# A hybrid decoder layer on one core: each 512-column product pass issued as two passes of 256 columns

## The chip, the cores and the metric

The kernel runs on one core of a Trainium2 chip. The metric is the device time of one execution, in microseconds (us). The profile is that of one execution; "span" is its time from the first to the last instruction. TensorE multiplies (its matrix multiplies stand in the profile as PE, its loads of the stationary operand as PEld), VectorE is DVE, ScalarE is ACT, GpSimd is POOL, and SyncE (SP) issues the DMAs.

## What is computed

One layer with a residual stream of 1024 tokens by 1024 features, all in float32:

```python
xn = rms_norm(h, mix_norm)
z  = xn @ W_in                  # q | k | v | gate_a | u | gate_s, 512 columns each
attn = dilated_mixture_attention(q, k, v) * silu(gate_a)       # 8 heads of 64
ssm  = s5_glu(u, ...) * silu(gate_s)        # 32 groups, 64 complex states, then a GLU
h  = h + concat(attn, ssm) @ W_out
h  = h + sigmoid(rms_norm(h, ple_norm) @ W_g) * (p @ W_p)
```

## The kernel before

Every dense product of two float32 operands is made of three passes, so that the rounding of one pass is made up by the others. Each operand is split into a high part (a copy in float32r, on ACT, L157 for weights) and a low part (the difference, on DVE or POOL, L158 for weights). The helper `mm3` (L106 to L109) then adds high x high, high x low and low x high in one PSUM bank of 512 float32 columns. Its arguments are the bank `o`, the stationary operand (`lh`, `ll`, 128 columns) and the moving operand (`rh`, `rl`, 512 columns). Every `matmul` becomes one load of the stationary operand and one multiply.

By the loops of the code `mm3` is called 696 times with 512 columns: 64 times for the state space input (tiles `u`), 128 for the two gates (`g`), 64 each for `q`, `k` and `v`, 32 for the GLU (`glu`), 64 for each half of the output projection (`os`, `oa`), 120 for the embedding gate (`gt`) and 32 for the embedding projection (`pe`). That is 2088 passes of 512 columns. Another 16 calls have 256 columns: the last feature tile of `gt` is cut into columns 0 to 512, 512 to 768 and 768 to 1024 (`LASTC`), so 48 passes of 256 columns stand at the end of the program.

The program runs through these stages: `u`; then the state space heads (many small DVE operations, a scan for each of the 32 groups in eight rounds, each round ending in the tile `xpv` on DVE, which PE multiplies into `yp` at L599 and, after a GELU on ACT, transposes at L608), with the 16 gate tiles `g` woven in, each of which DVE takes out of PSUM at L640; then `q` and `k`; then `v`, the GLU and the first half of the output projection `os`, with attention woven in (scores `sc` at L793 and L750, row minima on DVE at L780, exponentials on ACT at L803, a transposing DMA into `pt`, products `pv` at L818 and L824, and a transpose of each finished token block, `at`, at L763); then `oa`, and then `gt` and `pe`.

The order on each engine isn't written out by hand. The kernel is built by a scheduler that plays the program through with its own estimates of durations and lets each engine take what is ready first by them, with priorities given by hand. So a change in the number or size of the multiplies can move instructions on every engine. On the chip each engine keeps to the order that the scheduler left.

Of the kernel before, what the change touches and what calls it, by code (L numbers as in the profile page):

```python
# [58 lines left out]
PB = {"prb": (2, 2), "hl": (2, 2), "pt": (3, 2)}  # L59
# [18 lines left out]
def hybrid_layer(ctx: ExitStack, tc: tile.TileContext, a: dict, dbg=None):  # L78
    nc = tc.nc
    V, A, Q, T = nc.vector, nc.scalar, nc.gpsimd, nc.tensor  # L80
# [7 lines left out]
    def bank(tag, name, shape=(P, 512)):  # L88
        return ps.tile(list(shape), F32, tag=tag, name=name, bufs=BANKS[tag])
# [13 lines left out]
    yg_s = dr.tile([512, S], F32, name="yg_s")  # L103
    h_s = dr.tile([D, S], F32, name="h_s")

    def mm3(o, lh, ll, rh, rl, first, last):  # L106
        T.matmul(o, lh, rh, start=first, stop=False)  # L107
        T.matmul(o, lh, rl, start=False, stop=False)  # L108
        T.matmul(o, ll, rh, start=False, stop=last)  # L109

    def rsqrt(pool, v, shape, tag, steps=3):
        y = pool.tile(list(shape), I32, tag=tag + "y", name=tag + "y")
# [9 lines left out]

    ident = cp.tile([P, P], F32, name="ident")

# [1 line left out]
    wp = ctx.enter_context(tc.tile_pool(name="wp", bufs=4, side="right"))  # L126
    rp = ctx.enter_context(tc.tile_pool(name="rp", bufs=2, side="right"))
    ph1 = ExitStack()
# [63 lines left out]
    for k in range(KT):  # L192
# [15 lines left out]
        for j in range(6):  # L208
            f, n = divmod(j, 2)
# [13 lines left out]
    for k in range(KT):  # L223
        for n in range(2):
            mm3(acc[n], wu[k][0][:, 3 * P:], wu[k][1][:, 3 * P:], xh[k][:, n * 512:(n + 1) * 512],
                xl[k][:, n * 512:(n + 1) * 512], k == 0, k == KT - 1)
# [4 lines left out]
        stats(ss, "st1", rcol, rrow)  # L231
        V.tensor_tensor(rsq_, rcol, rcol, op=OP.mult)

# [1 line left out]
    def p16(name):  # L235
        return s1.tile([P, G, 16], F32, tag="p16", name=name, bufs=7)

# [28 lines left out]
    def named(n, shape=(P, G)):  # L266
        return s1.tile(list(shape), F32, name=n)
# [73 lines left out]
    are, aim = named("are"), named("aim")  # L341
# [28 lines left out]
    tt(w16, bre, bc(sci, 16), OP.mult)  # L370
    tt(bb, bb, w16, OP.add)

    # powers of A: PA = [Re; -Im], PB = [-Im; -Re]
    pa, pb = named("pa", (P, G, 9)), named("pb", (P, G, 9))
    for hf, (x0, y0) in enumerate(((1.0, 0.0), (0.0, -1.0))):
        hs = slice(hf * 64, hf * 64 + 64)
# [39 lines left out]
    tt(r8, r8, r8, OP.mult)  # L416
    tt(r8, r8, r8, OP.mult)

    # rotations e^{i 8 theta k}, k = 16 a + b; sine rows are [s; -s]
    e1c, e1s = csr, snr  # L420
    for j in range(3):
        e1c, e1s = csq(named(f"ec{j}"), named(f"es{j}"), e1c, e1s, norm=True)
# [27 lines left out]
    def feat_tile(w, f, n, tag, name):  # L450
        o = bank(tag, name)
        c = slice(n * 512, (n + 1) * 512)
        for k in range(KT):
            mm3(o, w[k][0][:, f * P:(f + 1) * P], w[k][1][:, f * P:(f + 1) * P],
                xh[k][:, c], xl[k][:, c], k == 0, k == KT - 1)
        return o
# [10 lines left out]
    for f in range(4):  # L467
        ust = [ev(f"ust{f}{e}", (P, 4, P)) for e in range(2)]
        for n in range(2):
            o = uraw[f][:, n * 512:(n + 1) * 512]  # L470
# [158 lines left out]
                ssm_store(f, ygt[f])  # L629
    sp.close()  # L630

# [1 line left out]
    for c0, dst in ((2560, sg_s), (1536, sa_s)):  # L633
        w = [load_w(wp, a["w_in"], k, c0, lo=GL) for k in range(KT)]
        for f in range(4):
            for n in range(2):
                o = feat_tile(w, f, n, "big", f"g{c0}{f}{n}")
# [5 lines left out]

    rrp.close()

# [1 line left out]
    kvp = ExitStack()  # L647
    def tok_tiles(w, bs, names, tag):
        os_ = [bank(tag, name) for name in names]
# [44 lines left out]
    for which, c0 in (("q", 0), ("k", 512)):  # L694
        w = [load_w(wp, a["w_in"], k, c0) for k in range(KT)]
        for bp in range(4):
# [3 lines left out]
            for b, o in zip(pair, tok_tiles(w, pair, [f"{which}{b}" for b in pair], QB[bp])):  # L700
                o = o.rearrange("p (h d) -> p h d", d=64)
# [14 lines left out]
            for b in (2 * bp, 2 * bp + 1):  # L716
# [10 lines left out]
                else:  # L727
# [1 line left out]
                    A.activation(hl[:, :, 0:64], raw, AF.Copy)  # L729
                    tt(hl[:, :, 64:128], raw, hl[:, :, 0:64], OP.subtract)  # L730
                    nc.sync.dma_start(ks[:, :, c], hl, transpose=True)
# [1 line left out]
    ma, ms_ = {}, {}  # L733

    def split(hi, lo, src, eng=Q):
# [138 lines left out]

    ph1.close()

# [1 line left out]
    rawp[0] = ctx.enter_context(tc.tile_pool(name="raw2", bufs=RAW[1], side="right"))  # L878
    mpx = ExitStack()
    mp = mpx.enter_context(tc.tile_pool(name="mp", bufs=6, side="right"))  # L880
# [20 lines left out]
    for n in range(2):  # L901
        c = slice(n * 512, (n + 1) * 512)
        ms_[n] = quad(f"msh{n}"), quad(f"msl{n}")
        for f in range(4):
            o = bank("big", f"glu{f}{n}")
# [14 lines left out]
                split(ms_[n][0][:, f], ms_[n][1][:, f], y, E[EM[f]])  # L920
            step(GS[4 * n + f])

# [1 line left out]
    def out_proj(part, src, scale, done):  # L924
        w = {}
        for sec in range(2):
# [64 lines left out]
    for sec in range(2):  # L991
        w = [load_w(wp, a["w_ple_gate"], k, sec * 512, gain=plen[:, k:k + 1]) for k in range(KT)]
        wq = [load_w(ep, a["w_ple_proj"], k, sec * 512, "pg", nbuf=24) for k in range(2)]
        for fi in range(4):
            f = sec * 4 + fi
            fs = slice(fi * P, (fi + 1) * P)
            last = f == 7
# [24 lines left out]
            if last:  # L1022
                proj()
                for c in LASTC:
                    o = bank("big" if c[0] % 1024 == 0 else "s", f"gt{f}{c[0]}")
# [21 lines left out]


def _w_in_columns():
    """The u section with the channels of a group ahead of its groups."""  # L1050
    n = np.arange(3072)
    n[2048:2560] = n[2048:2560].reshape(4, 8, 16).transpose(0, 2, 1).reshape(512)
    return n
# [24 lines left out]
def _layout(inputs):  # L1078
# [3 lines left out]
    def cols(v):  # L1082
# [6 lines left out]
        "ple_norm": cols(i["ple_norm"][0]),  # L1089
        "b_glu": cols(i["b_glu"][0]),  # L1090
        "w_in": c(i["w_in"][0][:, _w_in_columns()]),
        "w_glu": c(i["w_glu"][0]),
        "w_out": c(i["w_out"][0]),
# [32 lines left out]
```

## Time and profile before

| | |
|---|---|
| runs shown, us | 686.2, 688.59 (median), 693.06 |
| the profiled execution's span, us | 686.2 |
| PE busy | 92% of the span, 3836 multiplies |
| PEld busy | 72%, 3836 loads |
| DVE busy | 72% |
| ACT, POOL busy | 42%, 44% |
| mean granted clock of TensorE | 0.968 of 2.4 GHz |

Multiplies overlap each other in the pipeline and their ends are modelled, so a busy share of PE near 100% says that there is always one under way. The distance from one start to the next is what one costs in a dense row. A wait is put down to what came last before the waiting instruction could start.

### The profile page before, as it was taken

The numbers are of one execution on the slowest core, as the hardware profiler recorded it, in microseconds if no ns is written. First come the engines' busy times: TensorE is split into PE (matmuls) and PEld (weight loads), VectorE is DVE, ScalarE is ACT, GpSimd is POOL, SyncE is SP. The second block draws the span as 40 slices with busy tenths as digits, with TensorE's granted clock in tenths as the row PEclk, the third lists the DMA queues.
The fourth block names the chain that finished last, engine by engine and source line by source line (L and its number), as shares of the span: only waits on it lengthen the run. The fifth ranks groups of instructions, "written<-read, shape, count | busy, mean of one in ns | idle before, by whom it ended". The sixth has DMA issues, their size and how long they took to land.

```text
span 686.2 us, 10942 instructions
## 1 busy us (share of the span) xinstructions
PE 630.0 (92%) x3836; PEld 491.9 (72%) x3836; DVE 496.8 (72%) x1126; ACT 289.5 (42%) x553; POOL 302.0 (44%) x230
## 2 busy tenths in 40 slices
PE   9997799777879999999899789889999999999997
PEld 6875577566768788877677556566677888888786
DVE  6999999899998557767553998957944766626322
ACT  7532123445576624348434646534513455113100
POOL 3433825866775224234332845422432437342641
PEclk9999899998999999999999889989999999999999
DMA  7803612323444746754661868899987243015101
GB/s 257 241 7 109 209 38 76 105 79 93 77 92 92 167 69 125 159 86 125 161 122 48 216 147 148 213 192 191 217 226 244 94 152 124 15 63 165 50 32 61
DMA packets 158119, 87.25 MB, mean 127 GB/s; under 512 B 117232, under 2 KB 130416, under 8 KB 158064
## 3 DMA queue, kind: packets, MB, share of 16 engines
q1 hardware_dynamic: 158064, 86.56, 50.7%
q8 instruction: 30, 0.49, 0.3%
q14 instruction: 25, 0.20, 0.1%
HBM read 48.81 MB, written 17.27 MB: 96 GB/s over the span
## 4 chain that ended last, share of the span: by engine, by line
PE 46%; DVE 26%; DMA 12%; issue 7%; ACT 5%; POOL 2%; SPq 1%; DVEq 0%; ACTq 0%; POOLq 0%
PE gt L108 4%; PE gt L109 4%; PE gt L107 3%; DMA wr<-in_w_in 3%; DMA pt<-hl 3%; PE oa L107 2%; PE oa L109 2%; PE oa L108 2%; DVE tmp L270 2%; PE q L109 2%; PE q L107 2%; PE q L108 2%; DVE wl L158 2%; DVE p L780 2%; PE k L108 2%
## 5 line engine op out<-in xcount | busy, mean ns | idle before, releaser
L158 POOL TENSOR_TENSOR wl<-wr,wh 128x512 fp32r<-128x512 f32 x34 | 49.4, 1457 | 67.8 <-ACT wh L157 44.5
L157 ACT ACTIVATE wh<-wr 128x512 fp32r<-128x512 f32 x68 | 41.9, 626 | 51.4 <-DMA wr<-in_w_in 22.4
L810 POOL TENSOR_TENSOR hl<-p,hl 128x384 f16<-128x384 f32 (+2 forms) x34 | 38.9, 1148 | 53.9 <-ACT hl L807 27.1
L107 PE MATMUL g<-xh,wh 128*128 128x512 f32 x128 | 52.6, 411 | 7.3 <-DVE gate L640 5.5
L109 PE MATMUL g<-xh,wl 128*128 128x512 f32 x128 | 52.5, 410 | 5.3 <-DVE wl L158 5.3
L803 ACT ACTIVATE p<-p,st 128x384 f32<-128x384 f32 (+4 forms) x64 | 39.8, 622 | 39.1 <-DVE st L780 38.9
L108 PE MATMUL g<-xl,wh 128*128 128x512 f32 x128 | 52.0, 407 | 0.0
L108 PE MATMUL gt<-hl,wh 128*128 128x512 f32 (+1 forms) x136 | 51.7, 381 | 0.0
L107 PE MATMUL gt<-hh,wh 128*128 128x512 f32 (+1 forms) x136 | 51.7, 382 | 0.0
L109 PE MATMUL gt<-hh,wl 128*128 128x512 f32 (+1 forms) x136 | 51.2, 382 | 0.0
L158 DVE TENSOR_TENSOR wl<-wr,wh 128x512 fp32r<-128x512 f32 x34 | 34.8, 1025 | 19.1 <-ACT wh L157 14.0
L1016 ACT ACTIVATE gg<-gg 128x512 f32<-128x512 f32 (+1 forms) x17 | 10.1, 605 | 67.4 <-DVE gg L270 67.2
L1018 POOL TENSOR_TENSOR gg<-gg,hs 128x512 f32<-128x512 f32 x14 | 18.0, 1290 | 43.1 <-DVE gg L270 41.5
L107 PEld LDWEIGHTS g<-xh,wh 128*128 128x128 f32 x128 | 24.6, 192 | 13.7 <-DVE gate L640 6.5
L270 DVE TENSOR_TENSOR gg<-gt,rrow 128x512 f32<-128x512 f32 (+1 forms) x17 | 10.8, 656 | 32.7 <-PE gt L109 32.6
L109 PEld LDWEIGHTS g<-xh,wl 128*128 128x128 f32 x128 | 24.7, 193 | 12.0 <-DVE wl L158 6.6
L818 PE MATMUL pv<-vv,pt 128*128 128x64 f16 x504 | 24.4, 198 | 6.3 <-DMA pt<-hl 6.2
L818 PEld LDWEIGHTS <-pt 128*128 128x128 f16 x504 | 19.0, 101 | 14.8 <-DMA pt<-hl 8.9
L107 PEld LDWEIGHTS gt<-hh,wh 128*128 128x128 f32 x136 | 25.6, 188 | 5.5
L108 PEld LDWEIGHTS gt<-hl,wh 128*128 128x128 f32 x136 | 25.6, 188 | 5.4
L109 PEld LDWEIGHTS gt<-hh,wl 128*128 128x128 f32 x136 | 25.6, 188 | 5.4
L780 DVE CUSTOM_DVE_ANT_0 p<-sc,mask,gc 128x128 f32<-128x128 f32 (+3 forms) x56 | 24.3, 458 | 6.7 <-PE sc L793 3.2
(330 smaller groups left out, 1957.2 us busy)
## 6 DMA issues: line engine op xcount, KB each, us to landing
wr<-in_w_in SPq DMA_DIRECT2D x48, 256.0 KB, 2.9
xr<-in_x SPq DMA_DIRECT2D x16, 256.0 KB, 4.7
wr<-in_w_out SPq DMA_DIRECT2D x16, 256.0 KB, 3.3
xos<-in_x SPq DMA_DIRECT2D x16, 256.0 KB, 4.0
h_s<-xos SPq DMA_DIRECT2D x16, 256.0 KB, 3.4
xoa<-h_s SPq DMA_DIRECT2D x16, 256.0 KB, 2.8
wr<-in_w_ple_gate SPq DMA_DIRECT2D x16, 256.0 KB, 3.0
out_t<-gg SPq DMA_DIRECT2D x15, 256.0 KB, 2.0
```

The costliest lines, as they stand in the source:

```text
L107: T.matmul(o, lh, rh, start=first, stop=False)
L108: T.matmul(o, lh, rl, start=False, stop=False)
L109: T.matmul(o, ll, rh, start=False, stop=last)
L157: A.activation(hi, raw, AF.Copy)
L158: E[lo_on[k % len(lo_on)]].tensor_tensor(lo, raw, hi.bitcast(F32), op=OP.subtract)
L270: V.tensor_tensor(o, x, y, op=op)
L780: V.tensor_tensor_reduce(out, sc, msk, gm, init, op0=OP.add, op1=OP.min, accum_out=acc_[:, hd:hd + 1])
L803: A.activation(pb_, pb_, AF.Exp, bias=mx[:, hc], scale=-1.0, accum_out=dn[:, hc])
L810: E[LE[b][h0 % len(LE[b])]].tensor_tensor(hl[:, na:2 * na], pr_[:, 0:na], hl[:, 0:na], op=OP.subtract)
L818: T.matmul(pv[:, hd], pt[:, nf + i * nt + j + na * lp, :], vv[:, k0 + j, hd, lv, :], start=first, stop=end and not nf and j == n - 1 and l ...
L1016: A.activation(gt_, gt_, AF.Sigmoid)
L1018: (V if last else Q).tensor_tensor(gt_, gt_, hs, op=OP.add)
```

## The change

Where the output has 512 columns, `mm3` cuts the bank and the moving operand into two halves of 256 columns. Each of the three passes becomes two multiplies, the left half and the right half, which follow each other with the same stationary operand. Calls with fewer columns keep their three passes. A few comments go too, and all lines behind line 106 stand 13 lines lower.

```diff
+    def halves_of(x):
+        n = x.shape[1] // 2
+        return x[:, 0:n], x[:, n:2 * n]
+
     def mm3(o, lh, ll, rh, rl, first, last):
-        T.matmul(o, lh, rh, start=first, stop=False)
-        T.matmul(o, lh, rl, start=False, stop=False)
-        T.matmul(o, ll, rh, start=False, stop=last)
+        if math.prod(o.shape[1:]) != 512:
+            T.matmul(o, lh, rh, start=first, stop=False)
+            T.matmul(o, lh, rl, start=False, stop=False)
+            T.matmul(o, ll, rh, start=False, stop=last)
+            return
+        (o0, o1), (h0, h1), (l0, l1) = halves_of(o), halves_of(rh), halves_of(rl)
+        T.matmul(o0, lh, h0, start=first, stop=False)
+        T.matmul(o1, lh, h1, start=False, stop=False)
+        T.matmul(o0, lh, l0, start=False, stop=False)
+        T.matmul(o1, lh, l1, start=False, stop=False)
+        T.matmul(o0, ll, h0, start=False, stop=False)
+        T.matmul(o1, ll, h1, start=False, stop=last)
```

PE's program grows from 4804 to 6900 rows. The other engines keep their instructions, but in another order. Three places show it.

**The end of the state space heads, on PE.** The tiles `xpv_1681` (before) and `xpv_1873` (after) are those of the last scan round, and `yp` is the product that waits for them. Before, all 384 passes of the gates and 10 passes of `q` stand ahead of the first row with that `xpv`:

```order
L109 MATMUL g_2260<-xh_131,wl_1536_2054 128x512
L107 MATMUL q_2365<-wh_0_2318,xh_124 128x512
L108 MATMUL q_2365<-wl_0_2319,xh_124 128x512
L109 MATMUL q_2365<-wh_0_2318,xl_132 128x512
L107 MATMUL q_2365<-wh_0_2324,xh_125 128x512
L107 MATMUL q_2456<-wh_0_2318,xh_124 128x512
L108 MATMUL q_2456<-wl_0_2319,xh_124 128x512
L108 MATMUL q_2365<-wl_0_2325,xh_125 128x512
L109 MATMUL q_2365<-wh_0_2324,xl_133 128x512
L107 MATMUL q_2365<-wh_0_2330,xh_126 128x512
L109 MATMUL q_2456<-wh_0_2318,xl_132 128x512
L599 MATMUL yp_1699<-cp_1481,xpv_1681 128x128
```

In the changed program the last gate tile, `g_2812`, has only just begun there:

```order
L122 MATMUL g_2759<-xh_131,wl_1536_2438 128x256
L117 MATMUL g_2812<-xh_124,wh_1536_2395 128x256
L118 MATMUL g_2812<-xh_124,wh_1536_2395 128x256
L119 MATMUL g_2812<-xl_132,wh_1536_2395 128x256
L120 MATMUL g_2812<-xl_132,wh_1536_2395 128x256
L121 MATMUL g_2812<-xh_124,wl_1536_2396 128x256
L122 MATMUL g_2812<-xh_124,wl_1536_2396 128x256
L117 MATMUL g_2812<-xh_125,wh_1536_2401 128x256
L612 MATMUL yp_1891<-cp_1673,xpv_1873 128x128
```

Counted in passes of 512 columns from the start of the program, 586 stand ahead of this `yp` before and 555.5 after (192 of `u`, 360 of fifteen gate tiles, 3.5 of the last one): 30.5 fewer.

**The same place on DVE.** `gate` is a gate tile taken out of PSUM (L640 before, L653 after), `wl_0` is a low part of a weight of `q` (L158 and L171). Before:

```order
L640 TENSOR_TENSOR gate_2256<-g_2231,rrow 128x512
L578 SCALAR_TENSOR_TENSOR y_1673<-r_732,w_1669 128x128 x4
L584 MEMSET xpv_1681 128x4
L270 TENSOR_TENSOR xpv_1681<-y_1673,ec_1651 128x4x127
L158 TENSOR_TENSOR wl_0_2325<-wr_0_2322,wh_0_2324 128x512
L270 TENSOR_TENSOR xpv_1681<-xpv_1681,ysw_1678 128x4x127
L640 TENSOR_TENSOR gate_2285<-g_2260,rrow 128x512
```

After:

```order
L653 TENSOR_TENSOR gate_2755<-g_2706,rrow 128x512
L283 TENSOR_TENSOR w_1861<-w_1861,vs_1858 128x512
L591 SCALAR_TENSOR_TENSOR y_1865<-r_924,w_1861 128x128 x4
L597 MEMSET xpv_1873 128x4
L283 TENSOR_TENSOR xpv_1873<-y_1865,ec_1843 128x4x127
L283 TENSOR_TENSOR xpv_1873<-xpv_1873,ysw_1870 128x4x127
L653 TENSOR_TENSOR gate_2808<-g_2759,rrow 128x512
L171 TENSOR_TENSOR wl_0_2901<-wr_0_2898,wh_0_2900 128x512
```

From the start of the program to the last `xpv`, DVE has the same instructions in both programs but two: one `gate` and one `wl_0` have moved behind it.

**The end of attention, on PE.** `at` is the transpose of the last token block, `os` the first half of the output projection. Before, two tiles of `os` (24 passes) stand behind it:

```order
L108 MATMUL os_5422<-msl_3918,wh_512_4071 128x512
L109 MATMUL os_5422<-msh_3917,wl_512_4072 128x512
L763 MATMUL at_5951<-ident,atok_5947 128x128 x4
L107 MATMUL os_5628<-msh_3917,wh_512_4053 128x512
L108 MATMUL os_5628<-msl_3918,wh_512_4053 128x512
```

After:

```order
L119 MATMUL os_6520<-msl_5118,wh_0_5295 128x256
L120 MATMUL os_6520<-msl_5118,wh_0_5295 128x256
L776 MATMUL at_7391<-ident,atok_7387 128x128 x4
L121 MATMUL os_6520<-msh_5117,wl_0_5296 128x256
L122 MATMUL os_6520<-msh_5117,wl_0_5296 128x256
```

Counted as above, 1416 passes stand ahead of it before and 1391 after, 25 fewer; the first scores stand at 916 and at 915.5.

## Rows read from the trace of the kernel before

**Rows 1.** The profile's page: span, busy engines, chain that ended last, instruction DMA
```profile
span 686.2 us, 10942 instructions
...
PE 630.0 (92%) x3836; PEld 491.9 (72%) x3836; DVE 496.8 (72%) x1126; ACT 289.5 (42%) x553; POOL 302.0 (44%) x230
...
q8 instruction: 30, 0.49, 0.3%
...
PE 46%; DVE 26%; DMA 12%; issue 7%; ACT 5%; POOL 2%; SPq 1%; DVEq 0%; ACTq 0%; POOLq 0%
```

**Rows 2.** Busy time in stretches: start:end, length, busy us (instructions), clock, DMA, GB/s
```profile
core 0: us, PE busy (x) PEld busy (x) DVE busy (x) ACT busy (x) POOL busy (x), PEclk, DMA share, GB/s
15.00:225.00 210.00, 180.07 (x882) 144.94 (x881) 201.32 (x489) 93.07 (x170) 119.19 (x81) 0.95 0.38 102
225.00:305.00 80.00, 79.19 (x349) 63.87 (x350) 50.43 (x132) 32.45 (x50) 22.11 (x18) 1.00 0.60 119
375.00:455.00 80.00, 66.72 (x698) 45.71 (x698) 74.27 (x161) 45.22 (x101) 44.99 (x35) 0.89 0.81 182
455.00:514.00 59.00, 56.66 (x724) 40.48 (x722) 41.05 (x106) 22.75 (x48) 18.40 (x14) 0.95 1.01 206
514.00:682.00 168.00, 166.81 (x756) 135.24 (x754) 82.29 (x110) 49.28 (x79) 67.90 (x52) 1.00 0.30 102
```

**Rows 3.** Order of time, passes of 512 columns: start us, length us, engine, line, tiles
```profile
640.39 0.39 PE L108 MATMUL gt<-hl,wh 128*128 128x512 f32 x1
640.62 0.39 PE L109 MATMUL gt<-hh,wl 128*128 128x512 f32 x1
...
649.96 0.39 PE L107 MATMUL gt<-hh,wh 128*128 128x512 f32 x1
```

**Rows 4.** Order of time, passes of 256 columns and their loads, late and quiet
```profile
676.79 0.28 PE L107 MATMUL gt<-hh,wh 128*128 128x256 f32 x1
676.91 0.28 PE L108 MATMUL gt<-hl,wh 128*128 128x256 f32 x1
676.91 0.19 PEld L109 LDWEIGHTS gt<-hh,wl 128*128 128x128 f32 x1
...
677.02 0.28 PE L109 MATMUL gt<-hh,wl 128*128 128x256 f32 x1
677.02 0.19 PEld L107 LDWEIGHTS gt<-hh,wh 128*128 128x128 f32 x1
...
681.10 0.28 PE L109 MATMUL gt<-hh,wl 128*128 128x256 f32 x1
```

**Rows 5.** Order of time, the other passes of 256 columns, behind passes of 512
```profile
667.37 0.28 PE L107 MATMUL gt<-hh,wh 128*128 128x256 f32 x1
667.49 0.28 PE L108 MATMUL gt<-hl,wh 128*128 128x256 f32 x1
667.61 0.28 PE L109 MATMUL gt<-hh,wl 128*128 128x256 f32 x1
...
668.31 0.39 PE L107 MATMUL gt<-hh,wh 128*128 128x512 f32 x1
```

**Rows 6.** Order of time around the last xpv: what follows an idle time names its releaser
```profile
223.04 1.78 DVE L270 TENSOR_TENSOR xpv<-xpv,ysw 128x508 f32<-128x508 f32 x1
...
224.74 0.68 DVE L640 TENSOR_TENSOR gate<-g,rrow 128x512 f32<-128x512 f32 x1
224.87 0.49 PE L599 MATMUL yp<-cp,xpv 128*128 128x128 f32 x2 [0.30 <-DVE xpv L270]
```

**Rows 7.** Groups of instructions, DVE, 15 to 225 us: busy us, mean ns, idle before
```profile
L158 DVE TENSOR_TENSOR wl<-wr,wh 128x512 fp32r<-128x512 f32 x12 | 13.5, 1127 | 2.1 <-ACT wh L157 2.1
...
L640 DVE TENSOR_TENSOR gate<-g,rrow 128x512 f32<-128x512 f32 x16 | 10.9, 680 | 0.0
```

**Rows 8.** The chain that ended last, between 455 and 515 us, shares by line
```profile
by line: DMA pt<-hl 19.2%; PE os L107 10.0%; PE os L109 9.2%; PE sc L793 8.5%; PE os L108 8.5%; PE pv L818 7.4%; DMA h_s<-xos 7.0%; SPq L812 6.7%; DMA wr<-in_w_out 5.8%; PE pv L824 5.8%; PE at L763 3.5%; issue 2.4%; PE far L750 1.3%; PE sc 
```

**Rows 9.** Busy time of the tile os alone on PE, 455 to 515 us
```profile
455.00:515.00 60.00, 32.09 (x125) 0.95 1.00 206
```

## The prediction

> **What bounds the kernel now.** I read the page first, for which engine is the busiest. PE is busy 92% of the span, but the chain that ended last lies on PE for only 46% of it, and on DVE for 26% [rows 1]. So there are stretches with different limits, and the next view is the busy time by stretch [rows 2]. From 15 to 225 us, the state space heads, DVE works 201.3 of 210 us and PE has holes: DVE sets the pace. From 225 to 305 us PE is busy 79.2 of 80 us, and from 514 to 682 us 166.8 of 168: there PE sets it. From 375 to 455 us DVE is again the busier (74.3 of 80), and from 455 to 514 us no engine is full, while the DMA share is 1.01: the attention weave goes from one engine to the next.
>
> For the price of a pass I read start to start, not the modelled length. In a dense row of 512 columns, 41 steps lie between 640.39 and 649.96 us: 233.4 ns a pass [rows 3]. The program already holds passes of 256 columns with the same operands. Near the end 38 steps lie between 676.79 and 681.10 us, 113.4 ns each [rows 4]. The others, right behind passes of 512, take 0.94 us for eight steps, 117.5 ns each [rows 5].
>
> **What the change adds.** It turns 2088 passes into 4176, each with its own load of the stationary operand. That the second half uses the operand of the first saves no load: before, the first two passes of a call share one too, and there are still as many loads as multiplies, 3836 of each [rows 1].
>
> A pair of halves is therefore priced by the 256-column rows: at best 2 x 113.4 = 226.8 ns, 6.6 less than now. At worst I take the slowest two steps in a row, 667.37 to 667.61 us, 240 ns, 6.6 more than now [rows 5]. The 46 steps together, (38 x 113.4 + 8 x 117.5) / 46 = 114.1, make a pair 228.2 ns, and I take that: 5.2 ns less than one pass of 512. The bulk of the new work is dense rows like the 38, and they hold load and multiply one for one.
>
> The Trainium skill says otherwise in "TensorE: Matmul & The Clock Gate", section "Back-to-back issue gap": a warm multiply of N columns costs N/2.4 + 2.5 ns. By that the pair costs 2.5 ns more than one pass, since the fixed part is paid twice, and the sum below would end some 8 us later. The rows here disagree in both sizes: 233.4 ns against 215.8 for 512, and 113.4 against 109.2 for 256.
>
> Only passes in stretches that PE bounds turn this into time. In the changed order those are the 360 passes between the last `yp` (555.5) and the first scores (915.5), and the 697 behind the last `at` (1391) up to 2088. 1057 x 5.2 ns = **5.5 us less**; with the two ends, 7.0 less to 7.0 more. In the DVE-bound stretch a faster or slower pass is hidden by DVE.
>
> Instruction fetch grows: 30 DMA packets, 0.49 MB, feed PE's queue now, 0.3% of the DMA engines' time [rows 1]. That is 7672 loads and multiplies, 256 to a packet. Some 16 more packets are costed at nothing: PE uses one up in 128 steps, 30 us in a dense row now and 15 us then, so the next has long landed. Without that cover each would cost what it takes, 1.1 us (0.3% of 16 engines' 686 us, over 30), 18 us in all; the full stretches of PE show no such holes now [rows 2]. Evictions wait for the last half as they waited for the last pass: nothing.
>
> **What the change moves.** The scheduler left another order, and this is the larger part.
>
> First, the end of the state space heads. DVE has the same work ahead of the last `xpv` in both programs but for one `wl`, 1.13 us, and one `gate`, 0.68 us [rows 7]. If DVE stays as full as now, `xpv` lands 1.8 us earlier than at 224.8 us [rows 6], and no engine can bring it sooner than DVE's row allows, bar the 8.7 us in which DVE idles between 15 and 225 us [rows 2]. But PE has 30.5 fewer passes behind it when that `yp` runs: 20.5 of them are the rest of the last gate's tile, 10 are of `q`. From there PE is full for 80 us [rows 2], so what it did not do earlier it does now: 30.5 x 0.2334 = 7.1 us, less the 1.8: **5.3 us more**. The bounds are nothing, if DVE's idle time shrinks by as much, and 7.1.
>
> Second, the attention weave. 25 fewer passes stand between the first scores and the last `at`; they come behind it, where PE is full [rows 2]: 25 x 0.2334 = 5.8 us. Part of that comes back, since a pass taken out of the chain lets the chain end earlier. From 455 to 515 us the three lines of `os` make 10.0 + 9.2 + 8.5 = 27.7% of the chain [rows 8], 16.6 of 60 us, while 125 passes ran [rows 9], 29.2 us at 0.2334. So 57% of their time lay on the chain and comes back, 43% does not: 0.43 x 5.8 = **2.5 us more**, bounds 0 and 5.8.
>
> In both places PE waits in order. Behind a `yp` that waits for `xpv`, PE's whole queue waits, gates and `q` alike; that is why passes moved behind it are lost to the hole.
>
> **The sum.** 686.2 - 5.5 + 5.3 + 2.5 = 688.5 us, 2.3 above the span. The profiled execution is the fastest of the three shown, and their median is 688.59; 2.3 above that is **690.9 us**, 0.3% slower. A difference under 1% is about what a measurement of this kernel cannot tell from none: 681.7 to 695.5 us. The forecast's own range is 685 to 697.
>
> **The rivals.**
>
> *Each half pays its own overhead (slower).* A pass of 512 takes 20 ns more than its columns do at 2.4 GHz (213.3), a step of 117.5 takes 10.8 more than its 106.7. If every half costs 120, like the first two steps behind the 512s [rows 5], the pair is 240: 690.9 + 1057 x 11.8 ns = 703.4 us; at 117.5 throughout, a pair of 235.0, it is 698.1. The formula of the Trainium skill's page above lies near the second of these. Against it stand 38 steps of 113.4 [rows 4]; for it, that these ran while little else did, at the very end. It decides from a pair of 232.5 ns on: (695.5 - 690.9) / 1057 = 4.4 ns above 228.2. Chance 0.30.
>
> *The moved passes cost nothing (faster).* If the state space heads and attention end earlier by all that PE no longer does ahead of them, only the pair's price is left: 688.6 - 7.0 = 681.6 us at the best price, 683.1 at mine. For it: DVE has 8.7 us of idle time to lose. Against it: DVE is 96% busy there, and the work ahead is the same but for 1.8 us. Chance 0.21.
>
> *The loads become the bound (much slower).* Loads double. PEld is busy 491.9 us now; 2088 more of 0.19 us would make about 890, more than the span. Were a load to hold PE for its 0.19 us, a pair would cost 380 ns: 690.9 + 1057 x 152 ns = 851 us. Against it: in rows 4 loads of 0.19 us start every 0.11 us, so they overlap each other. Chance 0.03. The Trainium skill points this way: "Perfetto Trace Analysis", section "Identifying the Most-Contended Engine", takes the busy share of the loads for a good measure of how near TensorE is to its limit. Rows 4 show that in this form the summed length of the loads can exceed the time they take.
>
> That the halves are joined again is excluded, since both stand in the changed program's rows.
>
> **How the numbers follow.** The forecast has 0.46 (0.38 within 1%, 0.06 slower, 0.02 faster); the first rival 0.30 (0.27 slower, 0.03 within); the second 0.21 (0.11 faster, 0.10 within); the third 0.03, slower. So faster 0.13, within 1% 0.51, slower 0.36. The range goes from the second rival's 681.6 up to the first rival's 703.4, cut to 682 and 702, and leaves out the third and the tails of both. Predicted is the likeliest case, 690.9.
>
> **What would show it.** In the changed profile, 4176 more or less identical steps near 114 ns in the rows from 235 to 305 us and behind 520 us would confirm the price; 117 or more would confirm the first rival. Holes on PE between 90 and 225 us should be some 5 to 7 us larger, with the last `xpv` still near 223 us, and `q` should end that much later. Attention's last `at` should come at most about 3 us earlier after its first scores than now, with about 49 passes of `os` behind it. I am wrong if the last `xpv` comes by more than 5 us earlier or later, since then DVE's row was not the bound, if loads show up with waits of their own, or if halves of one pass stand apart in time.

## The result, and the profile after

The changed kernel is slower: 705.2 us in the median (702.4 to 710.8) beside 689.2 for the kernel before on the same chip. The ratio is 1.024, 95% interval 1.020 to 1.028. That lies above the range of the forecast (682 to 702), and more than 14 us above its 690.9.

The page of the profiled execution of the changed kernel, the lines that answer to [rows 1]:

```profile
span 704.5 us, 15115 instructions
...
PE 639.0 (91%) x5924; PEld 609.2 (86%) x5924; DVE 493.8 (70%) x1126; ACT 291.6 (41%) x554; POOL 301.6 (43%) x230
...
q8 instruction: 46, 0.75, 0.4%
...
PE 42%; DVE 32%; DMA 12%; issue 6%; ACT 3%; POOL 3%; SPq 3%; DVEq 0%; POOLq 0%; ACTq 0%
```

The span grew by 18.3 us, PE's busy time by only 9.0. The chain lies less on PE than before (42% against 46%) and more on DVE (32% against 26%). So PE at work is at most half of the growth. The 16 new instruction packets that the forecast counted are there (46 instead of 30).

Busy time in stretches, in the columns of [rows 2]; the last two are those that PE filled before:

```profile
core 0: us, PE busy (x) PEld busy (x) DVE busy (x) ACT busy (x) POOL busy (x), PEclk, DMA share, GB/s
15.00:225.00 210.00, 181.42 (x1407) 175.65 (x1406) 199.54 (x487) 93.64 (x170) 116.58 (x80) 0.94 0.41 100
225.00:305.00 80.00, 76.28 (x624) 75.86 (x623) 43.91 (x113) 28.65 (x43) 18.72 (x17) 0.96 0.62 120
...
514.00:682.00 168.00, 162.73 (x1415) 162.08 (x1411) 78.73 (x106) 50.62 (x80) 68.10 (x52) 0.99 0.37 116
```

From 15 to 225 us PE is as busy as before (181.42 us against 180.07), DVE a little less (199.54 against 201.32). In the other two PE was busy 79.19 of 80 and 166.81 of 168 us there, at a granted clock of 1.00 [rows 2]. Now it has holes of 3.7 and 5.3 us, at a clock of 0.96 and 0.99. The two largest holes are single waits. Here they are in the order of time on PE (start us, length us, and in brackets the idle time ahead and what ended it):

```profile
239.81 0.28 PE L122 MATMUL q<-wh,xl 128*128 128x256 f32 x1
243.80 0.58 PE L117 MATMUL q<-wh,xh 128*128 128x256 f32 x1 [3.72 <-ACT wh L170]
244.18 0.41 PE L118 MATMUL q<-wh,xh 128*128 128x256 f32 x1
...
599.88 0.93 PE L199 MATMUL st2r<-ident,col 128*128 128x128 f32 x5 [3.75 <-DVE col L195]
```

The first is `q` waiting for the last of its eight weight tiles. The second is `st2r`, the product that spreads the second norm's column over the partitions; it waits for `col`, which DVE computes. In the order of the kernel before 1730 passes stand ahead of `st2r`, in the changed order 1693.5 (a pair counted as one). PE reaches it sooner, too soon for DVE.

Two explanations stood against each other: the pairs cost the time, or the order does that the scheduler makes from them.

### The profile page after: what moved, and what is told of

Read it like the earlier page. It is cut to its first block, busy times and chain, and to the rows that moved or that the text cites. A ratio compares the mean times of both kernels' runs of the same rounds, so it can differ in the third digit from the quotient of the medians.

```text
span 704.5 us, 15115 instructions
## 1 busy us (share of the span) xinstructions
PE 639.0 (91%) x5924; PEld 609.2 (86%) x5924; DVE 493.8 (70%) x1126; ACT 291.6 (41%) x554; POOL 301.6 (43%) x230
## 4 chain that ended last, share of the span: by engine, by line
PE 42%; DVE 32%; DMA 12%; issue 6%; ACT 3%; POOL 3%; SPq 3%; DVEq 0%; POOLq 0%; ACTq 0%
DMA pt<-hl 4%; DVE tmp L283 3%; DMA wr<-in_w_in 3%; DVE w L283 2%; DVE p L793 2%; DVE wl L171 2%; PE gt L117 2%; PE gt L121 2%; PE gt L120 2%; PE gt L122 2%; PE gt L119 2%; PE gt L118 2%; DVE y L591 1%; DVE xpv L283 1%; DVE hl L822 1%
## 5 line engine op out<-in xcount | busy, mean ns | idle before, releaser
L171 POOL TENSOR_TENSOR wl<-wr,wh 128x512 fp32r<-128x512 f32 x34 | 49.7, 1463 | 65.2 <-ACT wh L170 58.3
L823 POOL TENSOR_TENSOR hl<-p,hl 128x384 f16<-128x384 f32 (+2 forms) x34 | 40.7, 1200 | 60.7 <-ACT hl L820 28.3
L171 DVE TENSOR_TENSOR wl<-wr,wh 128x512 fp32r<-128x512 f32 x34 | 32.0, 942 | 23.1 <-ACT wh L170 22.0
L117 PE MATMUL g<-xh,wh 128*128 128x256 f32 x128 | 37.7, 294 | 3.6 <-DVE gate L653 3.3
L121 PE MATMUL g<-xh,wl 128*128 128x256 f32 x128 | 37.8, 295 | 2.2 <-DVE wl L171 2.2
L120 PE MATMUL g<-xl,wh 128*128 128x256 f32 x128 | 38.3, 300 | 0.0
L118 PE MATMUL g<-xh,wh 128*128 128x256 f32 x128 | 38.1, 298 | 0.0
L122 PE MATMUL g<-xh,wl 128*128 128x256 f32 x128 | 37.9, 296 | 0.0
L119 PE MATMUL g<-xl,wh 128*128 128x256 f32 x128 | 37.6, 294 | 0.0
L120 PE MATMUL gt<-hl,wh 128*128 128x256 f32 x120 | 33.4, 279 | 0.0
L117 PE MATMUL gt<-hh,wh 128*128 128x256 f32 x120 | 33.3, 279 | 0.0
L122 PE MATMUL gt<-hh,wl 128*128 128x256 f32 x120 | 33.3, 277 | 0.0
L121 PE MATMUL gt<-hh,wl 128*128 128x256 f32 x120 | 33.3, 277 | 0.0
L118 PE MATMUL gt<-hh,wh 128*128 128x256 f32 x120 | 33.2, 277 | 0.0
L119 PE MATMUL gt<-hl,wh 128*128 128x256 f32 x120 | 33.1, 276 | 0.0
```

Source lines behind the costliest of these rows:

```text
L117: T.matmul(o0, lh, h0, start=first, stop=False)
L118: T.matmul(o1, lh, h1, start=False, stop=False)
L119: T.matmul(o0, lh, l0, start=False, stop=False)
L120: T.matmul(o1, lh, l1, start=False, stop=False)
L121: T.matmul(o0, ll, h0, start=False, stop=False)
L122: T.matmul(o1, ll, h1, start=False, stop=last)
```

## Experiments

A kernel here can be built with the instructions of one program in the order of another. The program is scheduled once for its order, then once more with every instruction tied behind the one ahead of it on its engine. The two halves of a pass are kept side by side. The core of it:

```diff
+    def build(cut, order=None):
...
+            hybrid_layer(tc, aps, cut, second)
+            rows = units(nc.cur_bb.bb.instructions, set(second))
+            for u, ahead in order or ():
...
+                    tc.add_manual_dep(y, x.name, mybir.DependencyInfo(
+                        mybir.DependencyClass.NoSync, mybir.DependencyReason.DATA), reason="order")
...
+    _, _, order = build(lambda o: False)
+    nc, arrays, _ = build(lambda o: True, order)
```

`cut` says which passes are split; the first `build` gives the order, the second the kernel that runs.

### The pairs alone, and the order alone

**e1**: all passes split, the order of before (the lines above).

> All 2088 512-column passes split as in the change, but every engine issues its instructions in the order of the kernel before, the two halves of a pass side by side. Order theory (the 18.3 us between the two spans come from the other order that the split made the scheduler choose; a pair costs about as much as the one instruction): span 686 to 690, ratio 0.999 to 1.006, st2r with no wait of 3.8 us ahead of it, the last wait of the gated products' first stage as before. Price theory (the pairs themselves cost it: 2088 x 8.8 ns = 18.3 us): span 702 to 706, ratio 1.022 to 1.029, the loss spread over all product stages in proportion to their passes.

Measured: 690.3 us, ratio 1.000 (0.998 to 1.003), span 685.7.

**e2**: no pass split, the order of the changed kernel.

```diff
-    _, _, order = build(lambda o: False)
-    nc, arrays, _ = build(lambda o: True, order)
+    _, _, order = build(lambda o: True)
+    nc, arrays, _ = build(lambda o: False, order)
```

> No pass split (512 columns in one instruction as before), but every engine issues in the order that the changed kernel has. Order theory: span 699 to 705, ratio 1.018 to 1.027, with the changed kernel's new waits in it (st2r waits about 3.8 us for col near 600 us, the first q pass waits about 3.7 us for its weights near 244 us). Price theory: span 685 to 689, ratio 0.998 to 1.005.

Measured: 710.1 us, ratio 1.028 (1.025 to 1.031), span 708.3. The order theory holds in both, and by itself: the pairs cost nothing that can be measured, and the order alone costs as much as the change. In the view of the tile `st2r` in e2, unsplit passes have the wait too (idle time of PE and PEld together, two times):

```profile
L199 PE MATMUL st2r<-ident,col x16: 275/421/422, 599.9 to 602.7; 128*128 128x128 f32 x16
...
  DVE col L195: 7.7, 2
```

```profile
L199 PE MATMUL st2r<-ident,col x16: 421/421/580, 601.8 to 605.2; 128*128 128x128 f32 x16
...
  DVE col L195: 7.6, 2
```

The first fence is the changed kernel, the second e2. The middle number of the first line is the median length: 421 ns, where 275 is the length without the wait (e4 below). Behind the wait the granted clock was 0.50, the lower of its two levels (1.2 of 2.4 GHz). In the changed kernel, in the columns of [rows 2]:

```profile
600.46:603.87 3.41, 3.41 (x19) 3.41 (x18) 2.05 (x3) 0.63 (x1) 0.00 (x0) 0.50 0.00 0
```

**e3**: only the 360 passes into `gt` split, the order of before.

```diff
-    nc, arrays, _ = build(lambda o: True, order)
+    nc, arrays, _ = build(lambda o: o.tensor.name.startswith("gt"), order)
```

> Only the 360 512-column passes into the gate tiles gt are split, in the order of the kernel before. In the changed kernel's trace the pair costs 227.4 ns there against 233.3 ns for the one instruction, in all other stages 2 to 9 ns more than the one instruction. If that price belongs to the operands of that stage: 360 x 5.9 ns = 2.1 us less, span 684.0, ratio 0.997. If the price of a half is the same everywhere and gt was only cheap through its neighbours in the other order (238 to 240 a pair): 1.6 to 2.4 us more, span 688, ratio 1.003.

Measured: 689.8 us, ratio 0.999 (0.997 to 1.001). Not told from no change. The dense steps into `gt` took 116.4 ns on the mean here, 114.5 in e1 and 113.6 in the changed kernel: the price of a half is not fixed by its operands alone. What else sets it stays open.

### Which places of the order

**e4**: the changed order, `st2r` and the first products into `pe` behind it 33 halves later.

```diff
+            a = next(n for n, u in enumerate(pe) if rows[u][0].outs[0].bass_ap.tensor.name.startswith("st2r"))
+            st2r, rest = pe[a:a + 8], pe[a + 8:]
+            gt, gp = ([u for u in rest if out[u] == x] for x in ("gt", "pe"))
+            by[mybir.EngineType.PE] = pe[:a] + gt[:33] + st2r + gt[33:52] + gp[:24] + gt[52:66] + rest[90:]
```

> The changed kernel in its own order, but the eight instructions into st2r stand 33 half passes into gt later on TensorE, and the 24 half passes into pe that follow them stand that much later too. Order theory: the wait of 3.75 us of st2r for col near 600 us goes, and with it the stretch at half clock behind it (3.4 us at half speed, 1.7 us): span 704.5 - 5.4 = 699, ratio to the kernel before 1.015 to 1.020. If the gated stage's end is set by something else (the stores behind pe, DVE): 703 to 705, ratio 1.022 to 1.027.

Measured: 701.3 us, ratio 1.016 (1.013 to 1.019). The view of `st2r` has no wait for `col` any more, and the length without it:

```profile
L199 PE MATMUL st2r<-ident,col x16: 270/275/275, 601.9 to 603.5; 128*128 128x128 f32 x16
```

The gain over the changed kernel, 1.024 less 1.016, is 0.8% or 5.7 us, as expected. This place is one cause.

**e5, e6, e15**: the order of before up to a seam, the changed order behind it; all passes split. The seams are the first `q`, the first `oa` and the first `k`.

```diff
+    n = next(i for i, u in enumerate(old) if tile_of[u].startswith("q0"))
+    head = set(old[:n])
+    nc, arrays, _, _ = build(lambda o: True, old[:n] + [u for u in new if u not in head])
```

> All passes split. Every engine issues in the order of the kernel before what stood there ahead of the first q product, and the rest in the order of the changed kernel. Of the changed kernel's 18.3 us, 8.0 had arisen by the last g product, 3.8 in q, k and v, 0.6 in the attention weave and 6.0 in oa, gt and pe. If the stages' losses are independent: the last g product ends near 222.4 (229.8 in the changed kernel), span 704.5 - 8.0 = 696.5, 694 to 699, ratio 1.011 to 1.018. If a later stage takes up what an earlier one loses: span 701 to 705. If the later losses follow from the first stage's: 686 to 690.

> All passes split. The order of the kernel before up to the first oa product, the order of the changed kernel behind it. Independent losses: 6.0 us in the last stage remain, of which st2r's wait near 600 us and the half clock behind it are 5.4: span 686.2 + 6.0 = 692.2, 690 to 694, ratio 1.006 to 1.011. If the last stage lost only because its inputs came late: 685 to 688, ratio 0.998 to 1.003.

> All passes split; the order of the kernel before up to the first k product, that of the changed kernel behind it (e5 had the seam at the first q product, where the q products then stood behind the last state-space products). If the place of the q products and of their inputs is what the first half of the program lost by: q ends near 272 as in the kernel before, and the losses left are the weave's 0.6 and the last stages' 6.0: span 691 to 694, ratio 1.006 to 1.011. If the later stages lose for themselves whatever comes before: 699 to 706.

Measured: e5 703.3 us, ratio 1.019 (1.014 to 1.024); e15 696.2, 1.010 (1.007 to 1.013); e6 693.4, 1.004 (1.001 to 1.006). So the old order of the state space heads alone brings no gain that is clear of noise: with their old order (e5) the last `g` ends at 222.4 as before, but `q` then starts at 228.6 instead of 222.5, since in the changed order the heads' last products stand ahead of it and wait for DVE. With the `q` products in their old place too (e15) more than half of the loss is gone. With the old order up to the first `oa` (e6) 0.4% is left, less than the 6 us read from the spans, although `st2r` still waits 2.6 us there.

**e11**, then **e13**: the changed order, other places on the SP queue. The queue in the changed kernel, in the order of time (start, length of the issue), and below it what DVE waited for:

```profile
225.34 4.88 SPq L165 DMA_DIRECT2D wr<-in_w_in  x4
230.34 3.68 SPq L626 DMA_DIRECT2D yg_s<-yo  x2
234.07 3.01 SPq L690 DMA_DIRECT2D gq<-in_q_norm  x1
237.43 0.34 SPq L691 DMA_DIRECT2D gk<-in_k_norm  x1
237.86 0.85 SPq L165 DMA_DIRECT2D wr<-in_w_in  x2
...
242.12 0.23 DVE L294 SCALAR_TENSOR_TENSOR gv<-gq,gk 128x64 f32<-128x64 f32 x1 [8.16 <-DMA wr<-in_w_in]
```

`gq` and `gk` are the gains of the norms of q and k, 32 KB each, and one of the two `wr` behind them is the last weight tile of `q`. All three stand behind two stores of `yg_s`; in the kernel before they stand ahead of them.

e11 moves the weight ahead of the stores, and nothing else:

```diff
+            sp = by[mybir.EngineType.SP]
+            wq = [u for u in sp if name(u).startswith("wr7_0_")]
+            sp.remove(wq[0])
+            sp.insert(sp.index(next(u for u in sp if name(u).startswith("gq"))) - 2, wq[0])
```

> The changed kernel in its own order, but on the SP queue the load of the last of q's eight weight tiles stands ahead of two stores of yg_s and the loads of gq and gk, as in the kernel before, instead of behind them. If this place makes TensorE wait 3.7 us for the weights near 240 us: the wait and the stretch at half clock behind it (1.8 us) go, span 704.5 - 5.5 = 699, ratio to the kernel before 1.014 to 1.020. If the load comes late anyway (its buffer, the queue's own backlog) or a later stage takes the gain: span 703 to 706, ratio 1.020 to 1.028.

Measured: 708.4 us, ratio 1.026 (1.024 to 1.028), no gain at all. The weight was early, but `q` then waited 6.3 us for its low part, which DVE makes behind `gv`:

```profile
244.30 0.23 DVE L294 SCALAR_TENSOR_TENSOR gv<-gq,gk 128x64 f32<-128x64 f32 x1 [10.77 <-DMA wr<-in_w_in]
```

DVE idled 10.77 us in front of `gv`. The bracket names the weight, but that had been issued by 232.8 us. `gk` was issued at 239.4 and took 4.5 us to land, which is 243.9: it was `gk`.

e13 moves all three:

```diff
+            g = next(n for n, u in enumerate(sp) if name(u).startswith("gq"))
+            by[mybir.EngineType.SP] = sp[:g - 2] + sp[g:g + 3] + sp[g - 2:g] + sp[g + 3:]
```

> The changed kernel in its own order, but on the SP queue the loads of gq, gk and of the last of q's weight tiles stand ahead of the two stores of yg_s, as in the kernel before, and not behind them. Theory of the stores: these two stores (4096 rows of 64 bytes each, 7.3 us to land) hold up gk, VectorE's gv stands ahead of the last wl and waits for gk, and so q's last product waits; in e11 only the weight went ahead, gk later still. Then the wait of 3.7 us near 240 us and the half clock behind it go: span 704.5 - 5.5 = 699, ratio 1.014 to 1.019. If it is the queue's backlog whatever the order: span 703 to 706, ratio 1.021 to 1.027.

Measured: 697.3 us, ratio 1.012 (1.009 to 1.014). The queue of e13 and DVE's `gv`:

```profile
230.69 0.42 SPq L690 DMA_DIRECT2D gq<-in_q_norm  x1
231.22 0.36 SPq L691 DMA_DIRECT2D gk<-in_k_norm  x1
233.31 0.33 SPq L165 DMA_DIRECT2D wr<-in_w_in  x1
233.98 3.57 SPq L626 DMA_DIRECT2D yg_s<-yo  x2
...
235.65 0.23 DVE L294 SCALAR_TENSOR_TENSOR gv<-gq,gk 128x64 f32<-128x64 f32 x1 [1.35 <-DMA wr<-in_w_in]
```

`gv` starts 6.5 us sooner than in the changed kernel, PE has no wait in `q`, and the last `q` starts at 275.3 instead of 281.7. The gain is 1.3%, some 8.7 us, and the second cause is this place on the SP queue: three loads behind two stores. In the changed kernel PE waits for the weight itself, which lands at 243.1 us; with the weight alone ahead it waits for what stands behind `gk` (e11). The two small loads ahead alone were not run.

**e14**: e13 and e4 together.

> The edits of e13 and e4 together in the changed kernel. If the two waits are independent: 704.5 - 5.5 - 5.4 = 693.6, ratio 1.004 to 1.011. If a later stage takes the first gain up: as e4, span 699 to 702, ratio 1.013 to 1.019.

Measured: 694.1 us, ratio 1.005 (1.003 to 1.008). The two places add up: 1.9 of the 2.4% are gone. What is left, 0.5%, has a place too. e15 and e6 differ only in the order from the first `k` to the first `oa`, and that is 1.010 against 1.004. From the first `sc` to the last `os` e14 takes 217.5 us, and the kernels with the old order there 211.5 to 214.9 (more on this stretch below). Which instructions of that stretch cost it was not found.

### Why the scheduler's order changed

Two guesses first. The leads by which the kernel marks work as urgent are given as a number of instructions, and a split pass counts twice. Or the scheduler reckons a pair longer than the one instruction.

**e7**: no pass split, but each counts twice. **e8**: all split, but a second half does not count.

```diff
+            if math.prod(o.shape[1:]) == 512:
+                tc.cur_priority += 3
```

```diff
+            p = tc.cur_priority
+            second.append(T.matmul(o1, l, r1, start=False, stop=sp).ins.name)
+            tc.cur_priority = p
```

> No pass split, but each 512-column pass counts twice in the program's running number, from which the scheduler takes priorities (their leads are given as a number of instructions), as the split made it. The scheduler then makes its own order. Theory of the leads (the order went wrong since 3000 instructions of lead now reach fewer passes): span 699 to 706, ratio 1.018 to 1.028. Theory of lengths (the order went wrong since the scheduler reckons a pair longer than the one instruction): span 685 to 692, ratio 0.998 to 1.008. Theory that any other order than the old one loses: between them and above, 692 to 699.

> All passes split, but a second half does not advance the program's running number, so that the scheduler's leads reach as many passes as in the kernel before; the scheduler makes its own order. Theory of the leads: span 685 to 692, ratio 0.998 to 1.008. Theory of lengths: span 699 to 706, ratio 1.018 to 1.028, with st2r waiting for col again. Theory that any other order loses: over 692.

Measured: e7 690.3 us, ratio 1.000 (0.997 to 1.002); e8 708.9, 1.027 (1.023 to 1.032). The leads are not it. The expectations then leave the lengths, but the orders themselves speak against those: scheduled with passes cut to 480 columns, 6% shorter, `st2r` stands behind 1731 passes, and with 512 behind 1730 (a count in the order alone, no run). A small change of length does not move it by 36. And e10, below, loses without any pair. What doubled is the count of instructions, and the scheduler has a number that counts them: it reckons that 35 instructions are handed over to TensorE ahead of the one that runs, and an instruction that becomes ready goes behind them. As halves these are 17.5 passes instead of 35.

**e9**: the changed kernel with 70 for this number. **e10**: the kernel before with 18.

```diff
+    depth = TRN2Spec.ENG_ISSUE_QUEUE_DEPTH
+    was, depth[mybir.EngineType.PE] = depth[mybir.EngineType.PE], 70
     with tile.TileContext(nc, schedule_with_timeline_sim=True) as tc:
         hybrid_layer(tc, aps)
+    depth[mybir.EngineType.PE] = was
```

> The changed kernel with one number of the scheduler altered: while it makes the order it reckons that up to 35 instructions stand handed over to TensorE ahead of the one that runs, so an instruction that becomes ready goes behind those 35. As halves they are 17.5 passes, whole ones 35. Here the number is 70. Window theory (this number times the split moved the small dependent products ahead of passes): st2r again stands about 30 passes later in the order and waits under 1 us for col, gp no longer waits 7.0 us for g near 84 us; span 686 to 693, ratio 0.999 to 1.010. If the order went wrong through the reckoned length of a pair: span 700 to 706, ratio 1.017 to 1.028.

> The kernel before, no pass split, with the scheduler's number of handed-over TensorE instructions at 18 instead of 35, the same number of passes as 35 halves. Window theory: the order is like the changed kernel's, st2r stands 36 passes earlier than in the kernel before and waits about 3.8 us for col near 600 us; span 699 to 708, ratio 1.018 to 1.030. If the split as such is needed for the loss: span 684 to 690, ratio 0.997 to 1.005.

Measured: e9 695.4 us, ratio 1.007 (1.004 to 1.009); e10 702.8, 1.019 (1.016 to 1.023). Both times lie where the window theory has them: the unsplit kernel with 18 loses most of what the split one does. In e9 `st2r` still waits 1.5 us, where under 1 was expected. In e10 the two places show again, `st2r` with a wait of 3.3 us on PE and `gv` with one of 7.5 us on DVE:

```profile
  DVE col L182: 7.1, 2
```

```profile
  DMA wr<-in_w_in: 7.5, 1
```

But no `q` product waits in e10, since q's last weight stands ahead of the stores there. The last `q` starts 3.0 us later than in the kernel before, not 10.9, and two of the first scores wait 1.0 and 1.5 us for DVE. So e10 shows that the number moves the order and costs about as much; it is not the changed kernel's loss wait for wait.

**e16, e12, e17**: the kernel before with 26, 70 and 50.

> The kernel before, no pass split, with the scheduler's number at 26. st2r now stands 21 passes earlier than in the kernel before (36 with 18), and gq and gk stand on the SP queue ahead of the last two stores of yg_s (behind them with 18). If the loss lies in those two places: st2r waits under 1 us (the changed kernel's wait of 3.75 us is 16 passes, 1693.5 + 16 = 1709.5), the q products wait for nothing: span 686 to 691, ratio 0.999 to 1.007. If the loss goes with the number evenly: half of e10's, ratio 1.007 to 1.013.

> The kernel before, no pass split, with the scheduler's number at 70: the small dependent products stand later still (st2r 22 passes later than in the kernel before). If an early small product costs a wait and a late one nothing: span 680 to 686, ratio 0.990 to 1.000. If late ones hold up the engines behind them as much: span 688 to 696, ratio 1.002 to 1.015.

> The kernel before, no pass split, with the scheduler's number at 50: gq, gk and all of q's weights ahead of the last stores of yg_s, st2r 22 passes later than in the kernel before. If only the two places count: within 1% of the kernel before, ratio 0.993 to 1.003, as with 70 (0.996). If the loss goes with the number evenly: faster than with 35 and slower than with 70, 0.996 to 0.999. If any other order loses: 1.005 to 1.02.

Measured, with the place of `st2r` counted in each order:

| number | passes | passes ahead of `st2r` | `gq`, `gk` against the last two `yg_s` | ratio (95%) |
|---|---|---|---|---|
| 18 (e10) | whole | 1694 | behind | 1.019 (1.016 to 1.023) |
| 35 (changed kernel) | halves | 1693.5 | behind | 1.024 (1.020 to 1.028) |
| 26 (e16) | whole | 1709 | ahead | 1.007 (1.004 to 1.010) |
| 70 (e9) | halves | 1723 | ahead | 1.007 (1.004 to 1.009) |
| 35 (before) | whole | 1730 | ahead | 1 |
| 50 (e17) | whole | 1752 | ahead | 1.004 (1.002 to 1.006) |
| 70 (e12) | whole | 1752 | ahead | 0.996 (0.993 to 0.998) |

The loss does not go evenly with the number: 50 is slower than 35, and 70 a little faster. Where both places are bad the kernel loses 2%; where they are better it lies between 0.4% faster and 0.7% slower. e16's 1.007 lies on the edge of both its theories, and e17's 1.004 just outside the first. The waits are not all gone there: `st2r` waits 1.5 us in e9, a `q` product 1.6 us in e16 (none was expected) and 0.5 us in e17, none in e12. Whether these few waits decide stays open. e12 is the one version that beats both kernels, by 0.4%, with unsplit passes.

## Why the prediction was wrong, point by point

**The price of a pair.** The forecast took 228.2 ns for a pair and 5.5 us of gain. In e1, where nothing but the pair differs, two dense rows in the order of time:

```profile
259.74 0.28 PE L121 MATMUL q<-wh,xl 128*128 128x256 f32 x1
...
269.95 0.28 PE L117 MATMUL q<-wh,xh 128*128 128x256 f32 x1
```

```profile
640.45 0.28 PE L119 MATMUL gt<-hl,wh 128*128 128x256 f32 x1
...
649.98 0.28 PE L119 MATMUL gt<-hl,wh 128*128 128x256 f32 x1
```

In `q` 86 steps take 10.21 us, 118.7 ns each, a pair of 237.4; one pass of 512 cost 234.2 there in the kernel before, on the mean of the dense steps. In this row of `gt` 84 steps take 9.53 us, 113.5 each, a pair of 226.9 against the 233.4 of [rows 3]. So the price read from [rows 4] was about right for `gt`, the tile that those rows belong to, and wrong for every other: on the means of e1's dense steps against the kernel before, a pair is 4.3 ns cheaper in `gt` and 2.3 (`v`) to 8.3 ns (`pe`) dearer elsewhere. Behind the last `os` this comes to 0.1 us as an estimate (192 x 4.4 in `oa` + 96 x 8.3 in `pe` - 360 x 4.3 in `gt`), and in `q` and `k` to 1.1 us; over the whole kernel e1 shows nothing, from 0.2% less to 0.3% more. The term of 5.5 us was not there. The step that failed is the sentence that the bulk of the new work is dense rows like those 38. The rule of the Trainium skill that the forecast weighed ("TensorE: Matmul & The Clock Gate", section "Back-to-back issue gap") makes a pair 2.5 ns dearer; that section gives the rule for a single multiply by itself. In sign the steps agree with it everywhere but in `gt`.

**The rival of overhead per half.** It gave 698.1 to 703.4 us and lay near the measured time, and its price of a half, 117.5 to 120, is what all tiles but `gt` show. But it isn't what made the kernel slower: in e1 the same pairs cost nothing in sum. That its time came near is luck.

**The end of the state space heads.** The last `xpv` was to land 1.8 us sooner than at 224.8. It started 1.3 us sooner and, being shorter (0.69 us against 1.78 [rows 6]), landed 2.4 us sooner:

```profile
221.77 0.69 DVE L283 TENSOR_TENSOR xpv<-xpv,ysw 128x508 f32<-128x508 f32 x1 [2.04 <-POOL ysw L600]
```

The last `g` started 8.0 us later than before. The forecast's 5.3 was for all 30.5 passes, the 10 of `q` among them; where the inputs of `q` come early, the last `q` starts 4.5 us (e13) and 2.2 us (e14) later than before, within the bounds. So PE does lag there, but not by the route that the forecast named. Its holes from 90 to 225 us were to grow by 5 to 7 us, and they shrank from 19.3 to 16.3. The kernel before and the changed one, in the columns of [rows 2]:

```profile
90.00:225.00 135.00, 115.74 (x613) 93.29 (x612) 128.33 (x227) 66.78 (x128) 84.66 (x56) 0.97 0.34 83
90.00:225.00 135.00, 118.68 (x933) 114.14 (x932) 125.21 (x235) 67.64 (x129) 82.62 (x55) 0.96 0.39 81
```

By 90 us 266 passes of `u` and `g` had started in the kernel before and 243.5 in the changed one: most of the lag is older than the last scan rounds. Between 65 and 90 us `gp`, a small product, waits 7.0 us for DVE there; the longest wait before was 4.2. That this wait makes the lag was not tried. The step that failed for the time is "from there PE is full for 80 us": the changed kernel is not full there. `q` lost another 2.9 us to its late inputs, and the last `q` started at 281.7 instead of 270.8. Removing the `q` wait in e13 brought back 6.4 of these 10.9 us.

**The attention weave.** 2.5 us were forecast; from the first `sc` to the last `os` the time went from 214.5 to 215.8, 1.3 more. These are single profiles, and the others say more. The four with the old order in this stretch (before, e1, e3, e6) took 211.5 to 214.9 us, the eight with the changed order (the changed kernel, e2, e4, e5, e11, e13, e14, e15) 215.8 to 219.7: 4.2 us more on the mean. So the term was there, and larger than forecast, within its bounds of 0 and 5.8. Its ends in e1, in the order of time on PE:

```profile
307.21 0.23 PE L806 MATMUL sc<-ks,qh 128*128 128x128 f16 x1
...
518.66 0.28 PE L122 MATMUL os<-msh,wl 128*128 128x256 f32 x1
```

Whether halves change this stretch isn't shown: in the old order split passes took 211.5 (e1) and 214.9 (e6), whole ones 214.5 (before) and 213.2 (e3). About 49 pairs of `os` were to stand behind the last `at`, and they do: from 521.0 to 532.6 us, 11.7 us at 237.6 ns.

**What was not looked at.** This is the step that failed most. The forecast said that the moved instructions were "the larger part", which is what the runs show. But it followed the new order on PE at two places only, and the sum took every other move at nothing. It did not go down the SP queue, where `gq` and `gk` had fallen behind two stores, nor through the last stages, where `st2r` stood 36.5 passes earlier. Both can be read from the order of the changed program before it runs. Those two places are 1.9 of the 2.4%. With both mended (e14) the kernel is 0.5% slower, near the forecast's 0.3%; that is luck in part, since its terms were -5.5, 5.3 and 2.5 us, where single profiles show about 0, 2 to 5, and 4.

**What held.** Instruction fetch cost nothing and the loads did not become the bound: e1 has the same 46 packets and 5924 loads (PEld 88% busy) and takes the time of the kernel before. Gate tiles were not taken out of PSUM too late: from 15 to 225 us PE waits 3.3 us for them in the changed kernel, and 5.5 before.

## What to carry to other kernels

Where a scheduler sets the order, an edit that changes only the number of instructions also changes the order on every engine, and here that was all of the effect that could be measured. Run the edit once in the old order and the old instructions once in the new order before saying what the edit costs. Before the run, go through the new order on each queue for small producers that many wait for: loads that fell behind large stores, and products that PE now reaches before their input is made.

## What the runs showed of the hardware that was not expected

A half of 256 columns has no one price: steps of 113.5 ns into `gt` and 118.7 into `q` in the same run (e1), 116.4 into `gt` on the mean of e3, where the passes around it are whole. The passes of 256 columns that the kernel before already has take steps of 113.4 ns in [rows 4], and 117.8 in e2 and e10, where no pass is split and they stand in another order. What sets it was not found.

Two stores of `yg_s` took 3.68 us to issue on the SP queue, and the load of `gq` right behind them 3.01, where ahead of them it took 0.42 (e13). So `gk` left 7.1 us after the first store began (230.34 to 237.43 in the changed kernel); it then landed 4.4 us later, about as ahead of them (4.3). A wait of 3.75 us on TensorE cost more than itself: the products behind it ran 421 ns instead of 275, at a granted clock of 0.50 for 3.41 us.
